# Weight sums on VectorE, an even share of plain products, and squares summed by TensorE in a two-layer hybrid decoder

## The chip, the cores and the metric

One Trainium2 chip, one core. The metric is the device time of one execution in microseconds (us); lower is better. Engines: TensorE (PE: matmuls; PEld: its weight loads), VectorE (DVE), ScalarE (ACT), GpSimd (POOL) and SyncE (SP, which here only issues DMAs).

## The reference

A decoder trunk of two layers on 512 tokens of width 1024, in float32. What matters here is the end of each layer:

```python
x = x + mixed @ w_out
h = rmsnorm(x, norm_mlp)
return x + jnp.square(jax.nn.relu(h @ w_up)) @ w_down   # w_up 1024x4096, w_down 4096x1024
...
return rmsnorm(x, norm_final)                             # after both layers
```

Ahead of it each layer projects the normed tokens and runs two attention mixers side by side: FoX (8 heads, with a forget gate whose logarithms are summed over the tokens) and NSA (compressed, selected and window branches, 8 heads on 2 key heads).

## The kernel before

Activations lie transposed, 128 features to a tile and 512 tokens along it, eight tiles `x[0]` to `x[7]`. A float32 product is made of three matmuls in the type fp32r: an operand is split into `h`, its rounded part (a cast on ACT), and `lo`, the rest (a subtraction on DVE); then h·h, h·lo and lo·h are summed in a PSUM bank. Every block of weights so costs a load, a cast and a split ahead of its matmuls.

**The MLP.** w_up is 32 blocks of 128 columns. The first 8 (`PLAIN`) are done plainly. The other 24 go in pairs, as 12 units `g` = 4 to 15, through a Strassen scheme: a unit has seven products (indices 0 to 6), each of four steps along the features, whose weight operands are sums of four 512-wide quarters of the two blocks: `r1` holds a11 and a12, `r2` holds s1 and a22. Of w_down, the first 3072 rows are done plainly in 48 products (`downs`, `D`), each of 12 matmuls, and their order is fixed by hand: 12 stand ahead of the units, then a table says how many go into each unit, at fixed places between its products (`between`), and what is left follows. The last 1024 rows of w_down go through Strassen again, as block pairs 16 to 19, with 28 products of 12 matmuls on 256 tokens each (`Strassen.down`, `first` and `second`). Units 13 to 15 (`slim`) work on 256 tokens at a time too, and give `combine` what pairs 16 to 19 need as right-hand sides.

**Sums of weights.** `load` brings a pair's two blocks, and three sums are needed: s1 = first half of r2 + its second half, s3 = first half of block 0 + first half of r1, and s2 = s1 + a11, which takes a11's place; then a12 takes in the new a11. In before, s1 and s3 are made by accumulating DMAs from POOL's queue (L1484; L1492 loads s3's first term and L1493 adds the second), s2 by DVE (L1283), a12 again by an accumulating DMA (L1289). Pairs 18 and 19 share the freed tiles of the right-hand sides, so their loads start only when unit 15 has given its last output: a copy of two columns on ACT (L1469) makes them wait.

**The last stage.** `operands` casts and splits one operand of pairs 16 to 19 for each product, seven ahead (L1285 on ACT, L1286 on DVE). A product is evicted into x by DVE (L1342 to L1363). Products s2, s3 and a22 accumulate onto the bank of an earlier one, so they wait for its eviction. In layer 0, `done` makes the next layer's operand from finished tiles of x (L268 on ACT, L269 on DVE) and sums their squares; in layer 1, `finish` squares and scales them, for the first 256 tokens (f = 0) and then for the rest (f = 1). `sumsq` squares on ACT and adds on POOL, or on DVE where `last` says so; `rstd` sums over the features with matmuls against ones (L301), makes the reciprocal root, and spreads it over the rows with matmuls (L318). `out` multiplies and writes: the first half's writing is interleaved with the last products.

**The queues.** The kernel writes instructions in program order for each engine; the build's scheduler may place one ahead of others of its engine where its own timing says so, and each engine then runs its list in order. SP issues all loads in its list's order, and one that waits for its buffer holds the ones behind it.

Of the kernel before, what the change touches and what calls it, by code (L numbers as in the profile page):

```python
# [11 lines left out]
F32 = mybir.dt.float32  # L12
F32R = mybir.dt.float32r
AF = mybir.ActivationFunctionType
OP = mybir.AluOpType
# [4 lines left out]
T = 512  # L20
# [117 lines left out]
def run(*gens):  # L138
    for g in gens:
        for _ in g:  # L140
            pass


class Body:
# [127 lines left out]
    def sumsq(self, x, acc, last=False):  # L272

        nc = self.nc
        n = x.shape[-1]
        s = self.t("tmp", [128, T], name="sq")[:, :n]
        nc.scalar.activation(s, x, AF.Square)
        if not acc:
            self.sums = 0
            return [s]  # L280
        if last == "apart":
            return acc + [s]
        self.sums += 1
        if self.sums == 6:
            self.table(AF.Sqrt, s)
        o = self.t("tmp", [128, T], name="acc")[:, :n]
        (nc.vector if last else nc.gpsimd).tensor_tensor(o, s, acc[0], op=OP.add)
        return [o]

    def table(self, f, after):  # L290

# [2 lines left out]
    def rstd(self, acc, tags=("O", "O"), wait=iter(()), exp=True, copy=True, R=None):  # L294

        nc = self.nc
        n = acc[0].shape[-1] // 128
        ps = self.p(tags[0])
        for b in range(n):
            for i, t in enumerate(acc):  # L300
                nc.tensor.matmul(ps[:, 2 * b:2 * b + 2], t[:, b * 128:(b + 1) * 128],  # L301
                                 self.ones2, start=i == 0, stop=i == len(acc) - 1)
        v, s, y, z = (self.t("s4", [128, NB], name=k)[:, :n] for k in "vsyz")
        nc.vector.tensor_scalar(v, ps[:, 0:2 * n:2], 1.0 / D, 1e-6, op0=OP.mult, op1=OP.add)
        nc.scalar.activation(s, v, AF.Sqrt)
        if exp:
            self.table(AF.Exp, s)
        nc.vector.reciprocal(y, s)
        nc.vector.tensor_mul(z, y, y)
        nc.vector.scalar_tensor_tensor(z, z, -0.5, v, op0=OP.mult, op1=OP.mult)  # L310
        rc = self.t("g4", [128, NB], name="rcol")[:, :n]
        nc.vector.scalar_tensor_tensor(rc, z, 1.5, y, op0=OP.add, op1=OP.mult)
        for _ in range(2):
            next(wait, None)
        def rows(tag):
            ps = self.p(tag)[:, :128 * n]
            for b in range(n):
                nc.tensor.matmul(ps[:, b * 128:(b + 1) * 128], rc[:, b:b + 1].to_broadcast([128, 128]), self.ident,  # L318
                                 start=True, stop=True)
            return ps  # L320

        ps = rows(tags[1])
        if not copy:
            R = self.t("r", [128, T], name="R")[:, :128 * n]
            nc.scalar.copy(R, ps)
            return rows(tags[2]), R
        if R is None:
            R = self.t("r", [128, T], name="R")[:, :128 * n]
        nc.scalar.copy(R, ps)
        return R, rc  # L330
# [57 lines left out]
        nc.vector.scalar_tensor_tensor(hl[:, 1], x, scale, hl[:, 0].bitcast(F32), op0=OP.mult, op1=OP.subtract)  # L388
        return hl

    def k_pair(self, x, fox=None, kd=None):


        hl = self.hilo(x, 1.0)
        if kd is None:
            t = self.t("kd", [128, 2, 2, T], F32R)
            kd = [t[:, 0], t[:, 1]]
        for e in range(2):
            for f in range(2):
                self.nc.sync.dma_start(kd[e][f * 64:(f + 1) * 64].bitcast(F32),  # L400
                                         hl[e * 64:(e + 1) * 64].bitcast(F32))
            if fox is not None:
                h = 2 * fox + e
                self.nc.sync.dma_start(kd[e][64:66, 1].bitcast(F32), self.CC[h:h + 33:32].bitcast(F32))
        return kd

    def q_pair(self, x, fox=False, keep=None):
# [447 lines left out]
    def layer(self, l, u):  # L855
        nc, a = self.nc, self.a
# [7 lines left out]
        g = self.token_proj(src, 512, va, u)  # L864
# [45 lines left out]
        def proj(i, key, fn, tag="mm"):  # L910
            def done(ps):
                st[key] = fn(ps)
            return self.block(wb[i], u, done, tag)
# [16 lines left out]
            return un  # L930

        def fox_proj(p, tags=("mm", "mm")):
            def keys(ps):
                if p == 0:
                    self.forget_sums()
                return self.k_pair(self.scaled(ps), p)

            yield from proj(2 * p, ("ka", p), keys, tags[0])
            yield from proj(2 * p + 1, ("qa", p), lambda ps: self.q_pair(self.scaled(ps), True), tags[1])

        def qproj(p):
            return proj(12 + p, ("qb", p), lambda ps: self.q_pair(self.roped(ps), keep=hl))
# [146 lines left out]
    def mlp(self, l, x, u, acc, gm):  # L1089
# [61 lines left out]
            if i == 8:  # L1151
                S.third(g0 + 1)
        run(conv)
        for g, n in zip(range(g0, 16), (2, 2, 3, 3, 4, 4, 4, 4, 4, 3, 1, 0)):
            for h in {14: (16, 17), 15: ()}.get(g, (g + 2,)):
                S.load(h)
            S.unit(g, D, n, acts)
            if g > 12:
                S.combine(g - 13)
# [78 lines left out]
class Strassen:  # L1238
# [33 lines left out]
    def operands(self, n):  # L1272

        b, nc = self.b, self.nc
        plan = self.plan()
        for k, g in plan[self.made:self.made + n]:
            self.made += 1
            r1, r2, s3 = self.raw[g]

            a11, a12, s1 = r1[:, :512], r1[:, 512:], r2[:, :512]  # L1280
            src = dict(a11=a11, a12=a12, s2=a11, s4=a12, s1=s1, a22=r2[:, 512:], s3=s3)
            if k == "s2":
                nc.vector.tensor_tensor(a11, s1, a11, op=OP.add)  # L1283
            h, lo = b.two("u2", "d")
            nc.scalar.copy(h, src[k])  # L1285
            nc.vector.tensor_tensor(lo, src[k], h.bitcast(F32), op=OP.subtract)  # L1286
            self.ops[k, g] = h, lo
            if k == "s2":
                nc.gpsimd.dma_start(a12, a11, accum_op=OP.add)  # L1289
            yield  # L1290
# [14 lines left out]
    def down(self, acts):  # L1305
# [63 lines left out]
        def finish(m, f):  # L1369
            xm = x[m][:, f * 256:(f + 1) * 256]  # L1370

            acc[f] = b.sumsq(xm, acc[f], ("sum", "apart")[f] if m == 7 else f and m > 4)
            nc.scalar.activation(xm, xm, AF.Copy, scale=b.gain[:, 32 + m:33 + m])

        def done(h, f):
# [11 lines left out]
        if not last:  # L1387
            b.load_small(l + 1)
            for g in (16, 18):
                if g == 18:  # L1390
                    b.ahead()
                run(first(g), second([(k, g + i) for k, i in self.LATE]))
            b.acc = acc
            return u
# [66 lines left out]
    def load(self, g, third=True):  # L1461

        b = self.b
        if g == 18:
            r = b.t("vn", [128, 2, 1024], name="raw")
            self.rest = [b.t("q2", [128, 2, 512], name="raw") for _ in range(3)]

            for t in [r] + self.rest:
                self.nc.scalar.copy(t[:, :, :1], self.c[3][:, :, :1])  # L1469
            r2, r1 = r[:, 0], r[:, 1]  # L1470
            s3 = self.rest[0][:, 0]
# [5 lines left out]
        else:  # L1477
            r2, r1 = (b.t("e", [128, 1536], name="raw") for _ in range(2))
            s3 = r1[:, 1024:]
        r1, r2, s3 = self.raw[g] = r1[:, :1024], r2[:, :1024], s3[:, :512]  # L1480
        for i, t in enumerate((r2, r1)):
            self.nc.sync.dma_start(t, self.source(g, i))
            if t is r2:
                self.nc.gpsimd.dma_start(r2[:, :512], r2[:, 512:], accum_op=OP.add)  # L1484
# [198 lines left out]
```

## Time and profile before

| | us |
|---|---|
| median of 3 runs | 1525.49 (1524.57 to 1527.33) |
| the profiled execution's own time | 1524.19 |
| its span, first to last instruction | 1522.2 |
| PE busy | 1499.7 (99%) |
| DVE busy | 1147.4 (75%) |
| ACT busy | 835.8 (55%) |
| POOL busy | 197.9 (13%) |
| mean granted PE clock | 0.996 |

Read it from the span: an engine that is busy 99% of it sets the pace nearly everywhere, and what is left to find are the few places where it waits or is slowed. Busy time of PE is modelled from pipelined matmuls, so it is not all work at full speed; which engine ended a wait is told by the list of waits, and what stood behind that by the chain of work and the timeline. The stretches (a table of busy times between two moments) show which engine was full there, the clock that was granted to PE and the share of the DMA engines.

### The profile page before, as it was taken

What the parts mean: (1) busy time and instruction counts of PE and PEld (TensorE: products, weight loads), DVE (VectorE), ACT (ScalarE), POOL (GpSimd) and SP (SyncE); (2) the same over time, 40 slices, a digit from 0 to 9 for tenths busy, and PEclk for the clock granted to TensorE, in tenths of its full rate; (3) what the DMA queues carried; (4) which work ended last, traced back from release to release, by engine and by line L of the source; (5) the groups of instructions that cost most, each with busy time, mean ns of one, the idle gap of its engine ahead of it and who ended that gap; (6) DMA issues with size and microseconds to landing.
All of it is one profiled execution on the core that took longest, in us unless ns stands there. A gap on an engine that the chain in (4) does not pass through costs nothing.

```text
span 1522.2 us, 22068 instructions
## 1 busy us (share of the span) xinstructions
PE 1499.7 (99%) x7952; PEld 1272.4 (84%) x7952; DVE 1147.4 (75%) x2204; ACT 835.8 (55%) x1588; POOL 197.9 (13%) x206
## 2 busy tenths in 40 slices
PE   9999999999999999999999999999999999999987
PEld 8888888888888888889988788888888888888987
DVE  5678979777488777789746799787674968777875
ACT  6465655554464655556545556555544636555655
POOL 4010000001200222222220000000011002221222
PEclk9999999999999999999999999999999999999999
DMA  7555422127324555455356552322452245555451
GB/s 270 168 161 132 132 70 79 61 94 226 103 89 144 135 153 138 138 150 149 90 196 173 153 143 76 91 73 70 139 187 97 97 138 158 138 142 141 101 132 56
DMA packets 72188, 197.26 MB, mean 130 GB/s; under 512 B 9072, under 2 KB 10480, under 8 KB 72080
## 3 DMA queue, kind: packets, MB, share of 16 engines
q1 hardware_dynamic: 57824, 170.41, 36.3%
q0 software_dynamic: 10368, 18.88, 7.2%
q10 hardware_dynamic: 3888, 6.58, 1.2%
q8 instruction: 62, 1.02, 0.3%
q14 instruction: 46, 0.38, 0.1%
HBM read 149.62 MB, written 4.19 MB: 101 GB/s over the span
## 4 chain that ended last, share of the span: by engine, by line
PE 89%; DVE 5%; ACT 2%; issue 2%; DMA 1%; DVEq 0%; POOL 0%; SPq 0%; ACTq 0%; POOLq 0%
PE ps_mm L243 11%; PE ps_mm L244 11%; PE ps_mm L245 11%; PE ps_PT L245 3%; PE ps_PT L243 3%; PE ps_PT L244 3%; PE ps_O L1533 3%; PE ps_S L1533 3%; PE ps_O L607 2%; PE ps_PT L581 2%; PE ps_S L556 2%; PE ps_mm L1533 2%; PE ps_PT L1533 2%; PE ps_S L243 2%; PE ps_S L244 2%; PE ps_S L245 2%
## 5 line engine op out<-in xcount | busy, mean ns | idle before, releaser
L217 ACT CAST wh<-raw 128x1024 fp32r<-128x1024 f32 (+2 forms) x177 | 181.8, 1027 | 234.5 <-PE ps_mm L244 68.0
L218 DVE TENSOR_TENSOR wl<-raw,wh 128x1024 fp32r<-128x1024 f32 (+2 forms) x177 | 211.9, 1197 | 38.8 <-ACT wh L217 37.9
L243 PE MATMUL ps_mm<-u,wh 128*128 128x512 f32 x512 | 205.1, 401 | 0.0
L245 PE MATMUL ps_mm<-u,wl 128*128 128x512 f32 x512 | 201.8, 394 | 0.0
L244 PE MATMUL ps_mm<-u,wh 128*128 128x512 f32 x512 | 201.7, 394 | 0.0
L1512 DVE TENSOR_TENSOR s<-raw,s 128x512 fp32r<-128x512 f32 x168 | 136.2, 823 | 54.8 <-ACT s L1511 54.0
L1484 POOL DMA_DIRECT2D raw<-raw x32 | 28.2, 881 | 759.7 <-PE ps_mm L245 238.7
L1511 ACT CAST s<-raw 128x512 fp32r<-128x512 f32 x168 | 102.6, 620 | 27.9 <-PE ps_PT L1533 5.0
L245 PEld LDWEIGHTS ps_mm<-u,wl 128*128 128x128 f32 x512 | 96.3, 188 | 19.9
L243 PEld LDWEIGHTS ps_mm<-u,wh 128*128 128x128 f32 x512 | 96.6, 189 | 19.1 <-DVE E L457 0.8
L244 PEld LDWEIGHTS ps_mm<-u,wh 128*128 128x128 f32 x512 | 96.4, 188 | 16.5
L243 PE MATMUL ps_mm<-o,wh 128*128 128x512 f32 x276 | 109.3, 396 | 0.0
L245 PE MATMUL ps_mm<-o,wl 128*128 128x512 f32 x276 | 108.3, 392 | 0.0
L244 PE MATMUL ps_mm<-o,wh 128*128 128x512 f32 x276 | 108.0, 391 | 0.0
L585 ACT CAST pth<-ps_PT 128x384 fp32r<-128x384 f32 (+1 forms) x96 | 48.9, 512 | 64.7 <-PE ps_PT L581 64.6
L543 DVE CUSTOM_DVE_ANT_0 E<-ps_S,ct 128x384 f32<-128x384 f32 (+3 forms) x112 | 57.4, 515 | 31.0 <-PE ps_S L556 30.2
L544 ACT ACTIVATE E<-E,tiny 128x384 f32<-128x384 f32 (+3 forms) x112 | 65.5, 585 | 20.0 <-DVE tiny L543 19.8
L586 DVE TENSOR_TENSOR ptl<-ps_PT,pth 128x384 fp32r<-128x384 f32 (+1 forms) x96 | 56.9, 599 | 13.9 <-ACT pth L585 12.5
L243 PE MATMUL ps_PT<-o,wh 128*128 128x512 f32 x156 | 61.6, 395 | 1.4 <-DVE z L1581 1.4
L245 PEld LDWEIGHTS ps_mm<-o,wl 128*128 128x128 f32 x276 | 52.0, 188 | 11.3
L245 PE MATMUL ps_PT<-o,wl 128*128 128x512 f32 x156 | 61.1, 392 | 0.0
L244 PE MATMUL ps_PT<-o,wh 128*128 128x512 f32 x156 | 60.9, 390 | 0.0
(451 smaller groups left out, 3715.9 us busy)
## 6 DMA issues: line engine op xcount, KB each, us to landing
raw<-wb SPq DMA_DIRECT2D x64, 512.0 KB
raw<-wup SPq DMA_DIRECT2D x64, 512.0 KB
raw<-wd SPq DMA_DIRECT2D x48, 512.0 KB
raw<-raw POOLq DMA_DIRECT2D x72, 256.0 KB, 4.1
w<-w SPq DMA_DIRECT2D x32, 256.0 KB
kda<-hla SPq DMA_DIRECT2D x32, 256.0 KB
q2a<-hla SPq DMA_DIRECT2D x64, 128.0 KB
raw<-wo SPq DMA_DIRECT2D x16, 512.0 KB
```

The source lines that it names most:

```text
L217: nc.scalar.copy(h[:, :n], raw[:, :n])
L218: nc.vector.tensor_tensor(lo[:, :n], raw[:, :n], h[:, :n].bitcast(F32), op=OP.subtract)
L243: mm(ps, h[:, c], xh, start=start and i == 0, stop=False)
L244: mm(ps, h[:, c], xl, start=False, stop=False)
L245: mm(ps, lo[:, c], xh, start=False, stop=stop and i == ks - 1)
L543: nc.vector.tensor_tensor_reduce(e, ps, self.mask[:, T - n:], -1.0, BIG, OP.add, OP.min, mx)
L544: nc.scalar.activation(e, e, AF.Exp, bias=mx, scale=-1.0, accum_out=un["sm"][:, i:i + 1])
L585: nc.scalar.copy(h[:, e, :n], ps[:, :n])
L586: nc.vector.tensor_sub(lo[:, e, :n], ps[:, :n], h[:, e, :n].bitcast(F32))
L1511: nc.scalar.copy(h, src)
L1512: nc.vector.tensor_tensor(lo, src, h.bitcast(F32), op=OP.subtract)
L1533: mm = lambda o, w, x, **kw: self.nc.tensor.matmul(o, w, x, skip_group_check=True, **kw)
```

## The change

Four things, in both layers unless said otherwise.

1. For pairs 18 and 19, `load` only brings r1 and then r2. The sums s3 and s1 are made on DVE inside `operands`, s3 behind the cast of a11 and s1 behind that of a12. A copy of one column on ACT, from x[1] into s3, ties s3 to the first evictions. The cast of the next layer's first weights (`b.ahead()`, layer 0) is tied to x[0] in the same way.
2. The table of plain w_down products for units 4 to 15 is (2, 2, 3, 3, 3, ..., 3) where it was (2, 2, 3, 3, 4, 4, 4, 4, 4, 3, 1, 0); both sum to 34.
3. In `finish` (layer 1), the squares of tiles 6 and 7 (f = 0) and of 5, 6 and 7 (f = 1) are not added but handed to `rstd` as tiles of their own, whose matmuls sum them; tile 5 (f = 0) and tile 4 (f = 1) are added on DVE, the others on POOL. `rstd` takes all blocks of a tile before the next tile.
4. For the first pair of heads, `fox_proj` calls `forget_sums`, and copies its sums into the keys' tiles, after the first quarter of the q product, where both stood at the end of the k product. For the other pairs the copies still come between the k and the q product.

```diff
@@ sumsq
-        s = self.t("tmp", [128, T], name="sq")[:, :n]
+        s = self.t("zz" if last == "apart" else "tmp", [128, T], name="sq")[:, :n]
...
+        self.sums += 1
+        if self.sums == 6 and len(acc) == 1:
+            self.table(AF.Sqrt, s)
         if last == "apart":
             return acc + [s]
-        self.sums += 1
-        if self.sums == 6:
-            self.table(AF.Sqrt, s)
...
-        return [o]
+        return [o] + acc[1:]
@@ rstd
-        for b in range(n):
-            for i, t in enumerate(acc):
-                nc.tensor.matmul(ps[:, 2 * b:2 * b + 2], t[:, b * 128:(b + 1) * 128],
-                                 self.ones2, start=i == 0, stop=i == len(acc) - 1)
+        for i, t in enumerate(acc):
+            for b in range(n):
+                nc.tensor.matmul(ps[:, 2 * b:2 * b + 2], t[:, b * 128:(b + 1) * 128], self.ones2,
+                                 start=i == 0 and b == 0, stop=i == len(acc) - 1, skip_group_check=True)
@@ k_pair (its argument fox goes)
-            if fox is not None:
-                h = 2 * fox + e
-                self.nc.sync.dma_start(kd[e][64:66, 1].bitcast(F32), self.CC[h:h + 33:32].bitcast(F32))
@@ fox_proj
-            def keys(ps):
-                if p == 0:
-                    self.forget_sums()
-                return self.k_pair(self.scaled(ps), p)
-
-            yield from proj(2 * p, ("ka", p), keys, tags[0])
-            yield from proj(2 * p + 1, ("qa", p), lambda ps: self.q_pair(self.scaled(ps), True), tags[1])
+            yield from proj(2 * p, ("ka", p), lambda ps: self.k_pair(self.scaled(ps)), tags[0])
+            q = proj(2 * p + 1, ("qa", p), lambda ps: self.q_pair(self.scaled(ps), True), tags[1])
+            if p == 0:
+                next(q)
+                self.forget_sums()
+            for e, k in enumerate(st["ka", p]):
+                h = 2 * p + e
+                nc.sync.dma_start(k[64:66, 1].bitcast(F32), self.CC[h:h + 33:32].bitcast(F32))
+            yield from q
@@ mlp
-        for g, n in zip(range(g0, 16), (2, 2, 3, 3, 4, 4, 4, 4, 4, 3, 1, 0)):
+        for g, n in zip(range(g0, 16), (2, 2, 3, 3, 3, 3, 3, 3, 3, 3, 3, 3)):
@@ operands
             self.ops[k, g] = h, lo
+            if g > 17 and k == "a11":
+                nc.scalar.copy(s3[:, :1], self.x[1][:, :1])
+                nc.vector.tensor_tensor(s3, a11, s1, op=OP.add)
+            if g > 17 and k == "a12":
+                nc.vector.tensor_tensor(s1, s1, r2[:, 512:], op=OP.add)
@@ finish
-            acc[f] = b.sumsq(xm, acc[f], ("sum", "apart")[f] if m == 7 else f and m > 4)
+            acc[f] = b.sumsq(xm, acc[f], "apart" if m > 5 - f else m > 4 - f)
@@ down, layer 0
                 if g == 18:
+                    spot = [b.t(k, [128, 1024], F32R) for k in ("wh", "wl")]
+                    nc.scalar.copy(spot[0][:, :1], x[0][:, :1])
+                    b.spots = deque([spot])
                     b.ahead()
+                    b.spots = ()
@@ load
-            for t in [r] + self.rest:
+            for t in [r] + self.rest[1:]:
                 self.nc.scalar.copy(t[:, :, :1], self.c[3][:, :, :1])
...
+        if g > 17:
+            self.nc.sync.dma_start(r1, self.source(g, 1))
+            self.nc.sync.dma_start(r2, self.source(g, 0))
+            return
```

More of the change, by code (lines that the diff above doesn't have):

```diff
@@ L389, in hilo, with k_pair @@
         return hl
-    def k_pair(self, x, fox=None, kd=None):
+    def k_pair(self, x, kd=None):
         hl = self.hilo(x, 1.0)
```

## The prediction

> **What bounds the kernel now.** I read the page first: which engine fills the span, and which carries the chain that ended last.
>
> ```profile
> span 1522.2 us, 22068 instructions
> ...
> PE 1499.7 (99%) x7952; PEld 1272.4 (84%) x7952; DVE 1147.4 (75%) x2204; ACT 835.8 (55%) x1588; POOL 197.9 (13%) x206
> ...
> PE 89%; DVE 5%; ACT 2%; issue 2%; DMA 1%; DVEq 0%; POOL 0%; SPq 0%; ACTq 0%; POOLq 0%
> ```
>
> The reader should see two things. TensorE (PE) is the bound nearly everywhere, and no matmul of weight is removed, so the change can only give back time in which PE waits or runs slowly. And 1499.7 of 1522.2 us busy leaves 22.5 us, of which the start and the output's end take a good part: the whole prize is some ten microseconds. So the second view is the list of what PE waited for.
>
> ```profile
> PE ps_mm L1326 <- DVE x L1348: 3.7, 1, 3.7
> PE ps_O L1326 <- DVE x L1352: 2.0, 1, 2.0
> PE ps_PT L243 <- DVE z L1581: 1.4, 1, 1.4
> ...
> PE ps_O L1519 <- DVE x L1110: 0.4, 1, 0.4
> ...
> PE ps_S L812 <- DVE tiny L801: 0.3, 1, 0.3
> ```
>
> Two of these waits, 5.7 us, are at L1326, the Strassen products of w_down at the end of each layer, and they wait for evictions on VectorE (DVE). An eviction takes 0.4 us, so something stood in front of it. The third view, the chain in order of time, says what: first layer 0's end, then layer 1's.
>
> ```profile
> 717.73 7.17 DMA raw<-raw
> ...
> 725.09 0.17 DVE raw L1283
> ...
> 727.94 2.56 PE ps_PT L1326 x12
> ...
> 732.29 1.44 PE ps_PT L1326 x12
> ```
>
> ```profile
> 1467.22 6.24 DMA raw<-raw
> ...
> 1475.66 2.93 PE ps_mm L1326 x12
> ```
>
> The accumulating transfer (raw<-raw) makes s3 from r1; L1283, the sum for s2, overwrites r1's first half and must wait for it; DVE works in order, so the evictions behind L1283 wait too, and PE with them. Then PE pays again: a product that takes 1.44 us takes 2.56 and 2.93. The stretches give the reason.
>
> ```profile
> 715.00:720.00 5.00, 4.13 (x35) 3.93 (x34) 5.00 (x10) 2.73 (x5) 2.11 (x3) 1.00 0.97 313
> ...
> 725.00:730.00 5.00, 3.74 (x23) 3.77 (x24) 4.19 (x8) 0.62 (x1) 1.14 (x2) 0.78 0.70 124
> ```
>
> ```profile
> 1450.00:1460.00 10.00, 8.57 (x62) 7.94 (x61) 9.93 (x16) 8.22 (x15) 2.09 (x3) 1.00 0.32 55
> ...
> 1475.00:1480.00 5.00, 4.34 (x25) 4.34 (x26) 3.76 (x8) 0.00 (x0) 1.74 (x2) 0.66 0.43 74
> ```
>
> The columns are length, busy time of PE, its weight loads, DVE, ACT and POOL, then the granted clock, the DMA share and GB/s. From 715 to 720 the DMA engines are full (0.97) while PE begins to starve; behind each wait the granted clock is down (0.78, 0.66). And from 1450 to 1460, in the last w_up unit of layer 1, DVE is full (9.93 of 10) and PE is not: that is the 1.4 us wait at L1581.
>
> **What the two ends lose**, from the timeline:
>
> ```profile
> 710.06 0.88 PE L1326 MATMUL ps_PT<-o,d 128*128 128x256 f32 x6
> ...
> 755.46 0.40 PE L360 MATMUL ps_S<-wh,u 128*128 128x512 f32 x1
> ```
>
> ```profile
> 1463.12 0.88 PE L1326 MATMUL ps_mm<-o,d 128*128 128x256 f32 x6
> ...
> 1479.96 1.60 PE L1326 MATMUL ps_mm<-tt,d 128*128 128x256 f32 x12
> ```
>
> Layer 0: 28 products at 1.44 us are 40.32; from the first to layer 1's first matmul it is 45.40, so 5.08 are lost. Layer 1: products 0 to 7 should take 8 x 1.44 = 11.52 and take 16.84, so 5.32 are lost. Wait and slow clock are both inside these.
>
> **Part 1: sums of blocks 18 and 19 on DVE.** In each layer four accumulating transfers (s1 and s3, twice) and two 256 KB loads leave; the four 512 KB loads stay, with r1 now first. The transfer that a12 takes after s2 stays too, but is wanted only by the late s4. Four sums of 128x512 join DVE. Their price, with that of a slot's other work:
>
> ```profile
> 720.17 0.43 DVE L1348 TENSOR_TENSOR x<-x,ps_O 128x256 f32<-128x256 f32 x1
> 720.50 0.70 DVE L1286 TENSOR_TENSOR d<-raw,d 128x512 fp32r<-128x512 f32 x1
> ...
> 727.69 0.69 DVE L1283 TENSOR_TENSOR raw<-raw 128x512 f32<-128x512 f32 x1
> ...
> 728.30 0.41 DVE L1352 TENSOR_TENSOR x<-x,ps_O 128x256 f32<-128x256 f32 x1
> ...
> 734.59 0.75 DVE L269 SCALAR_TENSOR_TENSOR u<-x,tiny,u 128x512 fp32r<-128x512 f32 x1 [0.40 <-ACT u L268]
> ```
>
> By start to start, an eviction holds DVE 0.33 us and a sum 0.61; a split (L1286) has the shape of a sum and I give it 0.61 as well. A product's slot of 1.44 us has one eviction and one split, 0.94. In the six slots of a11, a12 and s2 of 18 and 19 (L1283 was there before) it becomes 1.55, so DVE falls back 0.11 a slot, 0.7 us in all. Products accumulate onto a bank two slots after its last use, so one slot, 1.44 us, may be lost before PE sees it; splits are made seven products ahead. In layer 1 nothing more lies in these slots: hidden, and I keep 0.3 us for order. In layer 0 the same stretch, products 7 to 20, also holds four u splits (0.75 each), and the split of the next layer's first weights, which the change ties (by their cast) to x[0] and so moves here from the very start of the end:
>
> ```profile
> 713.24 1.22 DVE L218 TENSOR_TENSOR wl<-raw,wh 128x1024 fp32r<-128x1024 f32 x1
> ```
>
> DVE: 14 x 0.94 + 6 x 0.61 + 4 x 0.75 + 1.22 = 21.0 us in 14 x 1.44 = 20.2. Just full; I let 0.8 us show at PE. These weights are wanted at 755.46, some 20 us later, so their own delay costs nothing. The two dummy copies on ACT are one column wide; behind the one on s3 stand ACT's casts, but the eviction it waits for (of x[1]) is made five products earlier, or one in layer 1. Do the loads come in time?
>
> ```profile
> 1460.81 0.80 SPq L1482 DMA_DIRECT2D raw<-wdn  x2
> ```
>
> SP issued them 2.3 us before product 0 in layer 1. The accumulation at 1467.22 reads r1 of 18, so r1 is there 6.4 us after the issue at the latest, behind r2. As the first load it is no later, 4.1 us after product 0; a11 of 18 is cast after product 2, at 4.3. Part 2 puts one plain product more ahead of product 0, 2.7 us of margin. So the wait on a transfer goes, and the clock stays up. Gain: 5.08 - 0.8 = 4.3 in layer 0, 5.32 - 0.3 = 5.0 in layer 1. Ends: nothing of it (DVE takes the transfer's place) to all of it, 10.4 in both.
>
> **Part 2: three plain products to each unit.** The sum over units stays 34, two stay behind them, so PE's work is the same; five products a layer move from units 8 to 12 into 14 and 15. Can a unit with 256-wide products bear three? Unit 13 of layer 0 has three today:
>
> ```profile
> 663.28 1.43 PE ps_mm L1519 x12
> ...
> 681.58 1.43 PE ps_O L1519 x12
> ```
>
> 18.30 us, with 7 x 1.44 = 10.1 of its own: a plain product is 2.74, and PE lost nothing. In units 14 and 15 the three products buy 8.2 us each, and DVE, which was 9.93 of 10 full there, gets air. The 1.4 us wait at L1581 goes. What may come: unit 13 of layer 1, with three as well, had the 0.4 us wait at L1519, after this:
>
> ```profile
> 1417.07 2.53 DVE L1512 TENSOR_TENSOR s<-raw,s 128x512 fp32r<-128x512 f32 x1
> ...
> 1417.43 1.61 POOL L1645 TENSOR_TENSOR o<-z,o 128x512 fp32r<-128x512 f32 x1
> ```
>
> A DVE op of 0.69 took 2.53 while POOL computed. One in two such units at 0.4, over the four new ones, is 0.8 in the middle and 1.6 at worst. Its queues: the casts of weights, POOL's residuals and SP's loads for these products move with them, into units that load nothing (15) or two blocks (14). Gain 1.4 - 0.4 = 1.0, between -0.2 and 1.9.
>
> The Trainium skill (SBUF — State Buffer, Who interferes with whom) says that a VectorE instruction with two SBUF inputs contends with a GpSimd instruction that reads SBUF, and that the one issued later waits in full; the two rows above agree, and it speaks against part 1, whose sums have two SBUF inputs. By it each of the eight new sums could be stretched like that row, 8 x 1.84 = 14.7 us of DVE. At the two ends that would bring the first rival below, in units 13 to 15 the same rule brings the second; both are priced from rows, without the page.
>
> **Part 3: squares by TensorE.** For the first half of the tokens two tiles more, 2 blocks each, go through PE: four matmuls of two records.
>
> ```profile
> 1502.40 0.61 PE L301 MATMUL ps_PT<-tiny,acc 128*128 128x2 f32 x4 [0.38 <-DVE acc L287]
> ...
> 1511.20 0.41 DVE L287 TENSOR_TENSOR acc<-sq,acc 128x256 f32<-128x256 f32 x1
> ...
> 1511.54 0.41 DVE L1363 TENSOR_TENSOR x<-x,ps_S 128x256 f32<-128x256 f32 x1
> ...
> 1512.73 0.30 PEld L301 LDWEIGHTS ps_PT<-tiny,acc 128*128 128x128 f32 x2
> ...
> 1512.95 0.30 PEld L301 LDWEIGHTS ps_PT<-tiny,sq 128*128 128x128 f32 x2
> ```
>
> Two records take 0.22 (1512.73 to 1512.95), so that is +0.9 on PE, less the 0.38 wait for the add that goes: +0.5. For the second half the matmuls of the early tiles run before the last square, while PE waits anyway; behind it stand four records instead of six, -0.2, and the add at 1511.20 no longer stands before the last eviction at 1511.54, -0.3. Sum 0, between +0.5 and -0.5.
>
> **Part 4: forget sums and their copies.** Moved behind a quarter of the q product of the first pair, past its cast on ACT, its split on DVE and the next weights' load on SP. The wait at L812, 0.3 us, is covered by six matmuls. The first scores need q, whose product ends 18 matmuls later, so the small copies are covered; were they not, PE would wait for them once a layer, an SP issue's half of 0.80, 0.4. Gain 0.2, from -0.8 to 0.3.
>
> **The sum.** 4.3 + 5.0 + 1.0 + 0 + 0.2 = 10.5 us. The profiled execution took 1524.19 us (span 1522.2 and 2.0 around it), so the same would take 1513.7. The median of the runs shown is 1525.49, 1.3 above the profiled one; I forecast that median less 10.5: 1515.0.
>
> **The rivals.** (a) DVE takes the transfer's place: the build may order DVE's work otherwise than the program does (the split at 713.24 stands behind the whole first pair of blocks in the program and ran ahead of it), and with evictions behind sums and splits half of the ends' loss stays, 5.2 us, with the clock down again. For it: 21.0 in 20.2 us in layer 0. Against: layer 1 has room, and the splits are seven ahead. Gain 10.5 + 1.1 - 5.2 = 6.4: 1519.1. (b) The other side, slower: collisions of DVE and POOL in units 13 to 15. Each costs 2.53 - 0.69 = 1.84; a unit of 18.3 us has some 3 us of DVE to spare (DVE 84% busy in the row below), so from two collisions a unit the eviction of a plain product comes late and PE waits.
>
> ```profile
> 680.00:700.00 20.00, 20.00 (x149) 19.07 (x149) 16.87 (x22) 14.12 (x27) 6.09 (x5) 1.00 0.52 151
> ```
>
> With 2.3 us in each of the six units (three a layer), 13.8 against 10.5 gained: 1528.8. Against: POOL worked 6.09 of 20 us there, and PE still was 20.00. (c) The change doesn't do what it says: the loads of 18 and 19 themselves come late, since they start only after the last unit's output, and the ends lose as much as today; then parts 2 to 4 are left, 1.2 us: 1524.3. Against: 1.6 of the 4.2 MB moved there leave (six of the eight transfers of 256 KB that stand beside the four loads of 512), and 2.7 us of lead come.
>
> **How the numbers follow.** Forecast 0.72, (a) 0.14, (b) 0.07, (c) 0.07. About 0.2%, 3 us, is what a measurement here can tell from no change. Forecast and (a) are beyond it: faster 0.86; (c) is the same, 0.07; (b) slower, 0.07. The range goes from all the bounds at their good end (10.4 + 1.9 + 0.5 + 0.3 = 13.1, 1512.4, and 0.1% for the median) to past (a): 1511.0 to 1522.0. It leaves out (b) and (c).
>
> **What would show it.** Right: no raw<-raw transfer in the chain at the two ends, no wait at L1326 over 1 us, a granted clock of 1.00 in all stretches there, 28 products in 40.3 to 41.5 us, no wait at L1581. (a) shows as waits at L1326 for evictions with DVE full before them and no DMA; (b) as DVE ops over 2 us and bank waits in the units before; (c) as DVE or ACT idle for raw<-wdn. Wrong is the forecast if the ends keep more than 3 us of loss, or if a wait that is in no row here takes over 3 us.

## The result, and the profile after

| | before | after |
|---|---|---|
| median of 6 runs each, us | 1526.16 (1524.57 to 1529.58) | 1518.36 (1516.81 to 1519.51) |
| profiled execution, us | 1524.19 | 1519.51 |
| its span, us | 1522.2 | 1517.6 |

The ratio of the two is 0.9947, with a 95% interval of 0.9934 to 0.996: the change gains 7.8 us, where 10.5 were forecast. The two profiled executions are only 4.7 us apart: that of before lies 2.0 us under its median, that of after 1.2 us over its own. What follows is counted in the traces, so it has to add up to 4.6 us of span, and 3 us of the difference of the medians lie in no trace.

First the page of after: the span, the busy time of each engine, and the shares of the chain that ended last.

```profile
span 1517.6 us, 22072 instructions
...
PE 1500.4 (99%) x7968; PEld 1271.4 (84%) x7968; DVE 1153.4 (76%) x2211; ACT 836.6 (55%) x1590; POOL 190.3 (13%) x195
...
PE 87%; DVE 6%; ACT 3%; issue 2%; DMA 0%; POOL 0%; DVEq 0%; ACTq 0%; SPq 0%
```

DMA has gone from the chain (1% to 0%), PE's busy time is what it was. The list of what PE waited for, from its top, shows what is left:

```profile
PE ps_S L1547 <- ACT y L1610: 1.4, 1, 1.4
...
PE ps_mm L1547 <- DVE x L1109: 0.9, 2, 0.5
PE ps_mm L1331 <- DVE x L1353: 0.9, 1, 0.9
PE ps_mm L1533 <- DVE x L1109: 0.8, 1, 0.8
PE ps_PT L1547 <- ACT y L1610: 0.7, 3, 0.3
...
PE ps_mm L1547 <- ACT y L1610: 0.4, 1, 0.4
PE ps_O L1547 <- DVE z L1624: 0.4, 1, 0.4
...
PE ps_O L1547 <- ACT y L1610: 0.2, 1, 0.2
```

At the ends (L1331, L1326 before) 0.9 us remain of 6.6: the two waits that the prediction shows, 5.7, and a third one further down the list of before:

```profile
PE ps_PT L1326 <- DVE x L1348: 0.9, 1, 0.9
```

L1533 of after are the 256-wide products, L1547 the 512-wide products of w_up (L1533 in before, where that list has 1.0 us for ACT's copy `y` and nothing else). Six rows of after are at L1547, with 4.0 us: six waits for `y`, two for DVE's `x` (the eviction of a plain product, which frees its bank) and one for DVE's `z`. The prediction did not look at this place.

The stretches of the two ends (length, busy time of PE, weight loads, DVE, ACT and POOL, granted clock, DMA share, GB/s), two of layer 0 and one of layer 1:

```profile
718.00:723.00 5.00, 5.00 (x44) 5.00 (x44) 4.83 (x10) 2.14 (x5) 0.00 (x0) 1.00 0.00 0
...
738.00:743.00 5.00, 4.48 (x38) 4.27 (x36) 5.00 (x8) 2.87 (x5) 1.65 (x2) 1.00 0.26 102
...
1473.00:1478.00 5.00, 5.00 (x44) 5.00 (x43) 5.00 (x11) 2.06 (x5) 1.44 (x2) 1.00 0.04 8
```

The clock is 1.00 in all of them, and the DMA engines, 0.97 busy in a stretch of before, are at 0.26 or less. Only from 738 to 743, in layer 0, is PE short (4.48 of 5), and there DVE is full. The timeline shows what DVE carries:

```profile
730.29 1.23 DVE L218 TENSOR_TENSOR wl<-raw,wh 128x1024 fp32r<-128x1024 f32 x1
...
733.96 1.22 DVE L218 TENSOR_TENSOR wl<-raw,wh 128x1024 fp32r<-128x1024 f32 x1
...
739.11 1.29 POOL L287 TENSOR_TENSOR acc<-sq,acc 128x512 f32<-128x512 f32 x1 [0.74 <-ACT sq L277]
...
739.17 1.77 DVE L269 SCALAR_TENSOR_TENSOR u<-x,tiny,u 128x512 fp32r<-128x512 f32 x1
...
742.79 0.41 DVE L1353 TENSOR_TENSOR x<-x,ps_mm 128x256 f32<-128x256 f32 x1
743.35 0.83 PE L1331 MATMUL ps_mm<-tt,d 128*128 128x256 f32 x5 [0.87 <-DVE x L1353]
```

A u split that takes 0.75 us alone takes 1.77 beside POOL's sum of squares. That is not enough to make PE wait: in before the same split takes as long in the same place, and product 20, the one that waits 0.87 us here, waits 0.07 there.

```profile
739.70 1.78 DVE L269 SCALAR_TENSOR_TENSOR u<-x,tiny,u 128x512 fp32r<-128x512 f32 x1
```

What differs is the work in front. Here are the 14 us ahead of product 20, in before and in after:

```profile
729.88:743.88 14.00, 13.93 (x111) 13.76 (x111) 10.96 (x18) 8.71 (x14) 4.99 (x4) 0.95 0.32 96
```

```profile
729.35:743.35 14.00, 13.13 (x110) 12.95 (x109) 14.00 (x21) 9.41 (x15) 5.52 (x4) 1.00 0.66 189
```

DVE is busy for 10.96 us of them in before and for all 14.00 in after, where the tied cast has brought two splits of the next layer's weights (L218, 1.23 and 1.22) into it. The new sums are not there: the last of them ends at 725.7, and DVE idles once more, 0.20 us, just ahead of this stretch. With no slack left in it, the eviction that product 20 needs comes late.

**Where the time went, by stage.** From the start times of PE's matmuls each trace was cut at the same matmuls. "Loss" is what a stretch takes beyond its products at their unhindered pace (2.74 us for a plain product, 1.44 for one of the ends):

| stage | before | after | gain |
|---|---|---|---|
| first projections of layer 0, up to the first scores | 56.86 | 57.81 | -0.95 |
| 512-wide units, layer 0 (30 plain products, then 25) | 172.87 | 161.59 | -2.42, with the five products that left (13.70) taken out |
| 512-wide units, layer 1 | 172.36 | 161.24 | -2.58, the same way |
| units 13 to 15 and the two plain products behind them, layer 0 (in the units 4 plain products, then 9) | 46.94 | 60.51 | +0.13, with the five that came taken out |
| the same, layer 1 | 49.12 | 61.38 | +1.44, the same way |
| end of layer 0, loss | 5.08 | 1.10 | +3.98 |
| end of layer 1, loss | 5.32 | 0.0 | +5.32 |
| last eight products | 13.57 | 13.31 | +0.26 |
| from the last matmul of weight to the span's end | 11.42 | 11.74 | -0.32 |

The sum is +4.9, beside 4.6 of span. The ends gave the 9.3 us forecast. The units of w_up lost 3.4 us where part 2 was to gain 1.0. Not all of the 5.0 us in the 512-wide units come from the table: units 8 to 12, which gave a product each, take 92.78 and 92.97 us, where before less five products makes 90.93 in either layer, so they lose 1.9 and 2.0. The rest is unit 7's (1.3 longer, with units 4 to 6 0.2 shorter), which keeps its three products and their places; its length varies from trace to trace with either table (19.16 and 18.68 us in before, 19.79 and 19.34 in after, 18.59 to 19.74 in the eight runs below).

### The profile page after: what moved, and what is told of

It is laid out like the page before. It is cut to its first block, busy times and chain, and to the rows that moved or that the text cites. A ratio compares the mean times of both kernels' runs of the same rounds, so it can differ in the third digit from the quotient of the medians.

```text
span 1517.6 us, 22072 instructions
## 1 busy us (share of the span) xinstructions
PE 1500.4 (99%) x7968; PEld 1271.4 (84%) x7968; DVE 1153.4 (76%) x2211; ACT 836.6 (55%) x1590; POOL 190.3 (13%) x195
## 4 chain that ended last, share of the span: by engine, by line
PE 87%; DVE 6%; ACT 3%; issue 2%; DMA 0%; POOL 0%; DVEq 0%; ACTq 0%; SPq 0%
PE ps_mm L243 11%; PE ps_mm L244 11%; PE ps_mm L245 11%; PE ps_PT L243 3%; PE ps_PT L245 3%; PE ps_PT L244 3%; PE ps_O L604 2%; PE ps_PT L578 2%; PE ps_S L553 2%; PE ps_mm L1547 2%; PE ps_S L1547 2%; PE ps_O L243 2%; PE ps_S L243 2%; PE ps_O L244 2%; PE ps_S L244 2%
## 5 line engine op out<-in xcount | busy, mean ns | idle before, releaser
L217 ACT CAST wh<-raw 128x1024 fp32r<-128x1024 f32 (+2 forms) x177 | 181.7, 1027 | 228.1 <-PE ps_mm L244 63.8
L218 DVE TENSOR_TENSOR wl<-raw,wh 128x1024 fp32r<-128x1024 f32 (+2 forms) x177 | 219.3, 1239 | 40.4 <-ACT wh L217 39.8
L1526 DVE TENSOR_TENSOR s<-raw,s 128x512 fp32r<-128x512 f32 x168 | 129.7, 786 | 45.9 <-ACT s L1525 44.9
L1498 POOL DMA_DIRECT2D raw<-raw x28 | 24.6, 879 | 730.8 <-PE ps_O L604 240.0
L243 PE MATMUL ps_mm<-o,wh 128*128 128x512 f32 x256 | 101.0, 395 | 0.0
L245 PE MATMUL ps_mm<-o,wl 128*128 128x512 f32 x256 | 100.3, 392 | 0.0
L244 PE MATMUL ps_mm<-o,wh 128*128 128x512 f32 x256 | 100.2, 392 | 0.0
L245 PEld LDWEIGHTS ps_mm<-o,wl 128*128 128x128 f32 x256 | 48.2, 188 | 9.9
L243 PEld LDWEIGHTS ps_mm<-o,wh 128*128 128x128 f32 x256 | 48.2, 188 | 9.8 <-ACT o L494 0.4
L1284 ACT CAST d<-raw 128x512 fp32r<-128x512 f32 x56 | 34.1, 618 | 40.0 <-PE ps_mm L1331 9.9
L244 PEld LDWEIGHTS ps_mm<-o,wh 128*128 128x128 f32 x256 | 48.2, 188 | 9.1 <-DVE o L495 0.4
```

Source lines behind the costliest of these rows:

```text
L217: nc.scalar.copy(h[:, :n], raw[:, :n])
L218: nc.vector.tensor_tensor(lo[:, :n], raw[:, :n], h[:, :n].bitcast(F32), op=OP.subtract)
L243: mm(ps, h[:, c], xh, start=start and i == 0, stop=False)
L244: mm(ps, h[:, c], xl, start=False, stop=False)
L245: mm(ps, lo[:, c], xh, start=False, stop=stop and i == ks - 1)
L1526: nc.vector.tensor_tensor(lo, src, h.bitcast(F32), op=OP.subtract)
```

## The experiments

All were timed in five rounds against before, whose median was 1525.78 in the company of the first four and 1525.04 in that of the last four. The question is why the 512-wide units of after take 5 us more than those of before less the products that left. Theory A, cover: with four plain products a unit has one at each place (0, 1, 2, 3); with three they stand at (1, 2, 3), so none lies between products 1 and 2, and product 2, which adds to product 0's bank, waits for ACT's copy of it. Theory B is the prediction's part 2, which gives the table +1.0 and the wide units nothing. Theory C, lead, is about the ends: the even table shortens them, since it lets the loads of pairs 18 and 19 start earlier before the end's first product.

**The old table in the new kernel.**

```diff
-        for g, n in zip(range(g0, 16), (2, 2, 3, 3, 3, 3, 3, 3, 3, 3, 3, 3)):
+        for g, n in zip(range(g0, 16), (2, 2, 3, 3, 4, 4, 4, 4, 4, 3, 1, 0)):
```

> The changed kernel with the old table of plain products (part 2 undone, all else kept). Theory A (cover): in the changed kernel each 512-wide unit lacks the plain product between its products 1 and 2, so product 2 waits for ACT's copy of product 0's bank; these waits, about 2 us in layer 0 and 2.5 us in layer 1, go, and the wait at the end of unit 15 in layer 1 (1.4 us, 1.9 with the slow matmuls behind it) comes back: about 3 us faster than the changed kernel, 1515.5, with the two ends as short as in the changed kernel. Theory B (the prediction's part 2: the even table is worth 1 us): 1 us slower than the changed kernel, 1519.4, units without loss nowhere else. Theory C (the even table is what makes the ends short, by loads 2.7 us earlier): the ends lose 2 us or more each again, about 1521.

Measured: 1516.4 us, ratio 0.9943 (0.9931 to 0.9956). By the total it cannot be told from after (0.9934 to 0.996). By stage it can, though the profiled execution, at 1519.3 us, is the slowest of the five: the 512-wide units take 172.96 and 172.67, as in before, and units 8 to 12 exactly what they take there (104.63 in either layer), so their 1.9 and 2.0 us belong to the table. The old table pays elsewhere: its list of waits again has the 1.4 us of the last unit of w_up, and 1.2 us at the end of layer 0, whose loss is 2.57, where theory A had expected ends as short as in after. That end has its loads issued 0.5 us behind its first product, which is what theory C is about.

```profile
PE ps_PT L243 <- DVE z L1595: 1.4, 1, 1.4
...
PE ps_PT L1331 <- DVE x L1353: 1.2, 1, 1.2
```

**The even table alone, in before.** The same line, the other way.

> The kernel before with the even table alone (part 2 alone). Theory A: waits of 4 to 5 us at the starts of the 512-wide units of both layers, less 1.9 us at unit 15, ends unchanged but for the earlier loads: 1526 to 1529. Theory B: 1 us faster than before, 1525. Theory C: the ends lose 2.7 us less each, about 1521 or less.

Measured: 1519.3 us, ratio 0.9956 (0.9942 to 0.9969). The wide units again take 161.48 and 160.96, so no other part of the change makes them slow. But the table by itself gains 6.5 us, where the prediction gave it 1.0: with the transfers and sums all as in before, the loss of the ends falls from 5.08 to 0.29 in layer 0 and from 5.32 to 1.39 in layer 1. The timeline has SP's issue of the loads and the first product of each end:

```profile
707.56 0.80 SPq L1482 DMA_DIRECT2D raw<-wdn  x2
...
712.91 0.88 PE L1326 MATMUL ps_PT<-o,d 128*128 128x256 f32 x6
...
1455.86 0.81 SPq L1482 DMA_DIRECT2D raw<-wdn  x2
...
1461.21 0.88 PE L1326 MATMUL ps_mm<-o,d 128*128 128x256 f32 x6
```

The loads of pair 18 start 5.35 us ahead of the end in both layers; in before it was 2.3 in layer 1, and in layer 0 they were issued 1.1 us behind the first product. This fits theory C. Unit 15 now ends with a plain product of its own, so three of them, not two, lie between its last output and the end: 2.7 us more. In layer 1 that is nearly all of the added lead (3.0); in layer 0 it is less than half (6.5), and the rest means that unit 15's output itself came sooner.

**Part 1 alone, in before.** Sums on DVE, loads without transfers, and the tied cast.

```diff
...
+            if g > 17 and k == "a11":
+                nc.scalar.copy(s3[:, :1], self.x[1][:, :1])
+                nc.vector.tensor_tensor(s3, a11, s1, op=OP.add)
+            if g > 17 and k == "a12":
+                nc.vector.tensor_tensor(s1, s1, r2[:, 512:], op=OP.add)
...
+        if g > 17:
+            self.nc.sync.dma_start(r1, self.source(g, 1))
+            self.nc.sync.dma_start(r2, self.source(g, 0))
+            return
```

> The kernel before with the sums of blocks 18 and 19 on DVE alone (part 1 alone, with the tied cast of the next layer's weights). If part 1 stands on its own: the ends lose 1.1 us or less in each layer as in the changed kernel, 9 us less than before, 1517. Theory C: without the earlier loads a cast or a sum waits for raw<-wdn and the ends keep 2 us or more each: 1521.

Measured: 1517.46 us, ratio 0.9945 (0.9933 to 0.9958), a gain of 8.3. The loss of the ends is 1.49 and 0: with a lead of 0.6 us in layer 0 (loads at 709.36, first product at 709.95) and 2.3 in layer 1, the sums on DVE do what was predicted, and a little less than predicted in layer 0 (1.49 against 0.8). The wide units stay at 172.81 and 172.75, and the 1.4 us wait of the last unit stays too:

```profile
PE ps_PT L243 <- DVE z L1596: 1.4, 1, 1.4
...
PE ps_mm L1332 <- DVE x L1354: 0.9, 1, 0.9
```

Part 1 alone gains 8.3, the table alone 6.5, both (with the rest) 7.8: they cure the same stall, so they do not add up. With the sums on DVE the lead still matters in layer 0, but less: a lead of -0.5 us goes with a loss of 2.57 (the old table in the new kernel), 0.6 with 1.49 (here), 5.4 with 1.10 (after).

**The third plain product moved to place 0.** Only in the 512-wide units 8 to 12.

```diff
-        places = iter({1: (1,), 2: (0, 1), 3: (1, 2, 3), 4: (0, 1, 2, 3)}.get(n, ()))
+        places = iter({1: (1,), 2: (0, 1), 3: (0, 1, 3) if 7 < g < 13 else (1, 2, 3), 4: (0, 1, 2, 3)}.get(n, ()))
```

> The changed kernel with three plain products in each unit as before it, but in units 8 to 12 at places 0, 1 and 3 in place of 1, 2 and 3: one stands between products 1 and 2. Theory A: the waits for ACT's copy at the unit starts 8 to 12 go, 3 to 4 us faster than the changed kernel, about 1515. Rival (VectorE and GpSimd collide in these units wherever the plain products stand, or work is merely too much for 18 us): waits of the same size elsewhere in the units, 1518.

Measured: 1513.55 us, ratio 0.992 (0.9907 to 0.9932), 4.1 us better than after by the ratios. The same work in another order: the wide units fall to 158.73 and 158.99, against the 159.17 and 158.66 that before less five products makes. Units 8 to 12 alone, the only ones whose order was changed, take 90.89 and 90.88 us, against 92.78 and 92.97 in after and the 90.93 of before less five products. The timeline of after, at the start of a unit with three, shows the wait:

```profile
634.15 1.56 PE L1547 MATMUL ps_mm<-b,s 128*128 128x512 f32 x8
...
634.81 1.03 ACT L217 CAST wh<-raw 128x1024 fp32r<-128x1024 f32 x1
...
635.55 1.57 PE L1547 MATMUL ps_S<-t,s 128*128 128x512 f32 x8
635.75 0.63 ACT L1657 ACTIVATE y<-y 128x512 f32<-128x512 f32 x1
...
636.41 0.62 ACT L1658 CAST o<-y 128x512 fp32r<-128x512 f32 x1
...
636.93 0.58 ACT L1610 COPY y<-ps_mm 128x512 f32<-128x512 f32 x1
...
637.56 1.21 PE L1547 MATMUL ps_mm<-t,s 128*128 128x512 f32 x5 [0.45 <-ACT y L1610]
```

Product 0 is done at some 635.6, but ACT's copy of it begins at 636.93: a cast of weights (L217) and the square and the cast of the previous unit's output (L1657, L1658) stand in front of it. Product 1 covers 1.4 us and no more; product 2 waits. Here is the same unit in the kernel of this experiment:

```profile
631.63 1.56 PE L1547 MATMUL ps_mm<-b,s 128*128 128x512 f32 x8
633.03 1.57 PE L1547 MATMUL ps_S<-t,s 128*128 128x512 f32 x8
...
633.76 0.56 ACT L1610 COPY y<-ps_mm 128x512 f32<-128x512 f32 x1
634.44 0.40 PE L243 MATMUL ps_PT<-o,wh 128*128 128x512 f32 x1
...
637.22 1.56 PE L1547 MATMUL ps_mm<-t,s 128*128 128x512 f32 x8
```

The plain product at 634.44 lies between products 1 and 2; ACT's copy could end almost 3 us later and PE would not notice. The two kernels over the same 95 us of layer 0, first after, then this one:

```profile
560.00:655.00 95.00, 93.90 (x479) 78.56 (x478) 72.89 (x97) 56.83 (x96) 21.10 (x20) 1.00 0.55 149
```

```profile
560.00:655.00 95.00, 95.00 (x499) 80.83 (x499) 74.70 (x99) 56.83 (x98) 21.53 (x19) 1.00 0.53 147
```

ACT is as busy in both (56.83), PE has 1.10 us of gaps in the one and none in the other.

That the missing product at place 0 costs these units their 3.9 us is shown, and B is out: the three kernels with the even table at places 1, 2, 3 take 92.65 to 92.97 us for units 8 to 12, the three with place 0 take 90.86 to 90.95. The wait that theory A names is the larger part, not all: of the 2.0 us that the list of after has for these ten units, 1.2 are four waits of product 2 for ACT's copy, 0.4 is product 1's for DVE's eviction of a plain product, and 0.4 product 5's for DVE's `z`. The two waits for DVE go with place 0 as well; how was not traced. The two traces lie further apart than 3.9 us (5.8), partly because unit 7, left as it was, happened to be 1.2 us shorter in this one.

**The same with part 4 undone** (the forget sums and their copies where before has them).

```diff
...
-            q = proj(2 * p + 1, ("qa", p), lambda ps: self.q_pair(self.scaled(ps), True), tags[1])
-            if p == 0:
-                next(q)
-                self.forget_sums()
...
+            def keys(ps):
+                if p == 0:
+                    self.forget_sums()
+                return self.k_pair(self.scaled(ps), p)
...
```

> As e4_place0, with the forget sums and their copies back where the kernel before has them (part 4 undone). The stretch from a layer's first projection to its first scores took 56.8 to 57.4 us in layer 0 in the three kernels without part 4 and 57.5 to 58.5 in the three with it. If part 4 costs: 57.1 here and 0.5 to 1 us less than e4_place0 in all, 1513.0. If that was scatter: 57.5 or more again and 1513.5. The prediction (part 4 gains 0.2): 1513.8.

Measured: 1513.11 us, ratio 0.9921 (0.9909 to 0.9934): no difference. The first projections of layer 0 take 57.81, 58.47, 57.46 and 56.86 in the four kernels run with part 4, and 56.86, 57.40, 56.82, 56.89, 56.81 and 57.66 in the six without. The spread within each set is as large as what part 4 could bring; its effect stays unmeasured, and the 0.95 us that after lost there is not its doing as far as these runs can tell.

**Three plain products behind the units instead of two, in before.** One leaves unit 13 and stands behind, which tests theory C by itself: no sums on DVE, no even table, only more lead.

```diff
-        for g, n in zip(range(g0, 16), (2, 2, 3, 3, 4, 4, 4, 4, 4, 3, 1, 0)):
+        for g, n in zip(range(g0, 16), (2, 2, 3, 3, 4, 4, 4, 4, 4, 2, 1, 0)):
```

> The kernel before with one plain product of unit 13 moved behind the units: the table ends 2, 1, 0, so three stand between the last unit and the end's first product, where two stood. Nothing else changes. Theory C (lead: the ends stall because the loads of 18 and 19 start too late, so any work put between them and product 0 cures it): the loads leave 2.7 us earlier before product 0 and each end loses 2 to 3 us less: 1520.5. Rival (the ends got short with the even table because VectorE and ScalarE were no longer jammed by units 14 and 15): the loads still leave behind the jam, the ends lose 4 to 5 each: 1524 or more.

Measured: 1521.45 us, ratio 0.9969 (0.9958 to 0.9981), a gain of 3.6, between the 1520.5 of theory C and the 1524 of its rival. The profiled execution took 1517.89 us, the fastest of the six by 1.7, so the others may lose more at the ends than the trace shows. The loads and the first products of the two ends:

```profile
709.33 1.03 SPq L1482 DMA_DIRECT2D raw<-wdn  x2
...
711.74 0.88 PE L1326 MATMUL ps_PT<-o,d 128*128 128x256 f32 x6
...
1455.42 0.80 SPq L1482 DMA_DIRECT2D raw<-wdn  x2
...
1458.92 0.88 PE L1326 MATMUL ps_mm<-o,d 128*128 128x256 f32 x6
```

Lead and loss of each end, in this kernel between the two others:

| | before | three behind | even table alone |
|---|---|---|---|
| layer 0: lead, loss | -1.1, 5.08 | 2.4, 1.21 | 5.35, 0.29 |
| layer 1: lead, loss | 2.3, 5.32 | 3.5, 3.32 | 5.35, 1.39 |

More lead, less loss, in both layers: theory C holds as far as these traces go. The rival has a share in the lead itself. Three plain products lie behind unit 15's last output here and with the even table alone; yet there the lead is 2.9 and 1.9 us longer, so unit 15's output came sooner. The layers are not on one line (with 2.4 us layer 0 loses 1.2, with 2.3 layer 1 loses 5.3); why layer 1 needs more lead was not tried.

**The sums on DVE in the last layer alone**, with place 0 and without part 4: layer 0 keeps its transfers and the untied cast.

```diff
-            if g > 17 and k == "a11":
+            if g > 17 and k == "a11" and self.l + 1 == L:
...
-            if g > 17 and k == "a12":
+            if g > 17 and k == "a12" and self.l + 1 == L:
...
-        if g > 17:
+        if g > 17 and self.l + 1 == L:
             self.nc.sync.dma_start(r1, self.source(g, 1))
...
```

> As e5_no_move, with the sums of blocks 18 and 19 on VectorE in layer 1 alone; layer 0 makes them by accumulating transfers as before. With the even table alone layer 0's end lost 0.3 us with the transfers, in the changed kernel 1.1 with the sums on VectorE; layer 1's lost 1.4 with transfers, 0.0 with sums. If the two hold together: 0.8 us less than e5_no_move, and the fastest kernel here, 1512.3. If the transfers' slack in layer 0 hangs on the waits ahead (the units now run without them): layer 0's end loses 1 us or more again, 1513 or more.

Measured: 1512.84 us, ratio 0.9918 (0.9904 to 0.9932), the lowest of all; that it is lower than the two runs at 1513.11 and 1513.55 is not resolved. The loss of the ends is 0.29 and 0: with 5 us of lead layer 0 does better with the transfers than with the sums (1.08 to 1.10 in the four kernels with sums and even table). DVE is busy for 12.01 of the 14 us ahead of product 20, where after has 14.00, and product 20 waits 0.07 us. So the layer is better off without part 1 once it has that lead. The run undoes both the sums and the tied cast there. The trace of after points at the cast, since the sums are over before DVE fills up; a run that unties it and keeps the sums was not made.

**After without part 3** (squares summed as before).

```diff
...
-            acc[f] = b.sumsq(xm, acc[f], "apart" if m > 5 - f else m > 4 - f)
+            acc[f] = b.sumsq(xm, acc[f], ("sum", "apart")[f] if m == 7 else f and m > 4)
...
```

> The changed kernel with part 3 undone (squares added on GpSimd and VectorE as before). The last eight products and what follows them took 25.0 us before and 25.05 in the changed kernel's profile, 25.3 to 25.8 in two kernels without part 3, 24.4 to 25.1 in two with it. Prediction (part 3 is worth nothing, between -0.5 and +0.5): 25.0 to 25.5, 1518.4. Rival (it is worth more, since the wait for the added squares goes): 25.5 or more, 1519.

Measured: 1518.7 us, ratio 0.9955 (0.9942 to 0.9967), not to be told from after. Its last eight products take 13.57 us, and 13.56 or 13.57 in every kernel without part 3, 13.29 or 13.31 in every kernel with it: 0.26 us, seen in all ten traces and too small for the timed rounds. With what follows them it takes 25.91 us, on the side that the expectation gave to the rival (25.5 or more). The five kernels without part 3 take 24.99 to 25.91 for this, the five with it 24.33 to 25.08; the two ranges overlap, so part 3 may be worth more than the 0.26, and these runs do not settle it.

## Why the prediction was right, and where it was not

The time, 1518.4, lies inside the range and 3.4 us over the forecast. Some of that is luck: in the traces the terms add up to 4.9 of the 10.5 us, since part 2 had the wrong sign, and the 3 us that bring the medians to 7.8 lie in no trace. By its own figure for the profiled execution, 1513.7, the forecast is off by 5.8.

**Part 1 and the ends: right.** Forecast 4.3 + 5.0, measured 3.98 + 5.32. Of the signs named, no transfer is left in the chain at the ends, the clock is 1.00, no wait at L1331 exceeds 1 us, and layer 0's 28 products take 40.32 + 1.10 = 41.4 us, inside 40.3 to 41.5. The 0.8 us granted to layer 0 for a full DVE was 1.1 with the even table and 1.49 without it. The prediction's count of DVE's work, 21.0 us in 20.2, has one weight split of 1.22 in this stretch; two came, which is 1.2 more, and three instructions stretched beside POOL (1.80, 1.45 and 1.77, against 0.75, 0.69 and 0.75) add 2.8. What remains is rival (a) in small: 0.87 us behind DVE, no transfer involved. The rule of the Trainium skill (SBUF — State Buffer, Who interferes with whom) showed there: the split at 739.17, issued 0.06 us behind POOL's 1.29 us sum, took 1.77 instead of 0.75. Waiting in full would make 0.75 + 1.23 = 1.98, an estimate by that page; the trace gives a little less. The two rows that the prediction reads as agreeing show the collision but not that order: there DVE's record starts first (1417.07 against 1417.43) and is the one stretched. The eight new sums were not touched: each took 0.69 us. In layer 1, where no next layer's splits lie on DVE, no such delay reached PE.

**Part 2: the term that failed.** The step "PE's work is the same; five products a layer move from units 8 to 12 into 14 and 15" asked whether the units that receive can bear it, and answered rightly: +0.13 and +1.44, the 1.4 us wait gone, 0.8 us in one new wait. It did not ask what the units that give would lose. A plain product there was not only work, it was the cover between a bank's first product and the second that accumulates onto it. In units 8 to 12 that cost 1.9 and 2.0 us, against the 1.6 gained in units 13 to 15. (The rest of the 5.0 in the 512-wide units is unit 7's.) So the term is -2.3 where +1.0 was forecast. Both halves of this could be read in before. The timeline has product 2 of unit 7, one of the two 512-wide units with three plain products there, waiting 0.81 us for ACT's copy, and the start of a unit with four, where the copy of product 0's bank ends at 603.13, just ahead of product 1's end at 603.31, and could have ended 2.8 us later without PE noticing, because a plain product stands behind product 1 (product 2 starts at 605.93):

```profile
543.08 1.68 PE L1533 MATMUL ps_S<-t,s 128*128 128x512 f32 x8 [0.81 <-ACT y L1596]
...
600.34 1.56 PE L1533 MATMUL ps_mm<-b,s 128*128 128x512 f32 x8
601.74 1.57 PE L1533 MATMUL ps_S<-t,s 128*128 128x512 f32 x8
602.55 0.58 ACT L1596 COPY y<-ps_mm 128x512 f32<-128x512 f32 x1
603.15 0.40 PE L243 MATMUL ps_PT<-o,wh 128*128 128x512 f32 x1
```

Over the four such units of both layers the list of before has 1.0 us of waits for `y`, 0.25 a unit. Ten units more of that kind would lose 2.5 us by it, an estimate: two thirds of the 3.9 measured in them, and enough to turn the sign of this term.

**The sum treated the parts as separate.** The 2.7 us of lead from part 2 were noted, as margin for part 1. That they cure most of the same stall by themselves (6.5 us alone) was not. The forecast of the whole did not suffer, since the ends had been counted once; but rival (c), which left 1.2 us to parts 2 to 4 beside ends that lose as much as before, names a state that the lead of part 2 hardly allows, and a reader who wanted only one of the two parts would have been told that part 2 is worth 1.0.

**Rivals (b) and (c)** did not happen: units 13 to 15 lose nothing in layer 0 and gain in layer 1, and the loads of after start 5.4 us ahead of both ends (layer 1: 1458.40 against 1463.80).

**Parts 3 and 4** were sized 0 and +0.2. Part 3 gave 0.26 in the last eight products, within its bounds, and what it does behind them is not resolved; part 4 could not be seen.

**Open.** The first projections scatter by up to 1.6 us between kernels with the same code there, and the time behind the last matmul of weight by 1.3 us; both are as large as the small terms of the sum. Whether the tied cast alone makes the 0.87 us of layer 0, and how place 0 removes the two waits for DVE, was not tried.

## What to carry to other kernels

Independent work that is spread between dependent steps is cover; before moving a piece of it, look at what the step behind it waits for, on the giving side as much as on the receiving one, and find a place in the trace where that piece is already missing. Two edits that attack the same stall from its two sides (an earlier start, a shorter chain) were worth about the larger here, not the sum (6.5 and 8.3 us alone, 7.8 together), so price each alone and both together. A collision seen beside a wait need not be its cause: look for the same collision in a kernel where nothing waits. And where an engine carries the whole span, count gaps by stage from the start times of its instructions: losses of 0.2 to 0.7 us in seven of ten units made 3.9 us here, where the list of waits has 2.0 for them, mixed with those of a unit that the change did not touch.

## What the hardware showed that was not expected

The very end runs at one of two speeds. The four small matmuls that spread the reciprocal root (L318), after a wait of 1.3 us, took 0.71 us in before and 1.23 in after (0.71 or 0.74 in five of the other traces, 1.22 in three), with a granted clock of 1.00 and 0.85 in the stretch in which they begin. The timeline and the stretch of before, then of after:

```profile
1514.61 0.71 PE L318 MATMUL ps_O<-tiny 128*128 128x128 f32 x4 [1.27 <-DVE tiny L312]
```

```profile
1510.00:1515.00 5.00, 2.69 (x21) 2.32 (x20) 2.75 (x11) 2.48 (x7) 0.00 (x0) 1.00 0.38 131
```

```profile
1509.13 1.23 PE L318 MATMUL ps_O<-tiny 128*128 128x128 f32 x4 [1.28 <-DVE tiny L312]
```

```profile
1505.00:1510.00 5.00, 3.72 (x30) 3.64 (x30) 2.04 (x9) 2.06 (x5) 0.00 (x0) 0.85 0.39 134
```

The wait ahead is the same within 0.01 us. It is not part 3 that decides: without it one kernel (part 1 alone) took 0.71 and one (the table alone) 1.22. What does was not found. It is 0.5 us in these four matmuls; the whole time behind the last matmul of weight differs by 1.3 us between the ten traces.
